# The per-layer gate's product by seven block products, 512 columns wide, with the order of three engines by hand

## The chip, the cores and the metric

The kernel runs on one core of a Trainium2 chip. The metric is the device time of one execution in microseconds. Each kernel is run several times; the median stands for it. Besides, one execution is recorded by the hardware profiler, and the profile's numbers are of that one.

Engines of a core: PE (TensorE, matrix products and transposes through the identity; PEld is its weight load), DVE (VectorE), ACT (ScalarE), POOL (GpSimd), and SP, which here only issues DMAs.

## The reference

One decoder layer for a prompt of 1024 tokens and a sample of 8 sequences of 8 tokens, D_MODEL 1024, all in float32. Of its parts, mixer, MLP with convolution and per-layer input, the change touches the last, with the row scales that it needs:

```python
y, conv_new = conv_ffn(rmsnorm(h, lw['g_ffn']), conv_prev, lw)
h = h + y
h = h + (p.astype(h.dtype) @ lw['ple_w_proj']) * jax.nn.sigmoid(rmsnorm(h, lw['g_ple']) @ lw['ple_w_gate'])
```

`h` is 1024 x 1024 for the prompt (and 64 x 1024 for the sample), `p` 1024 x 256, `ple_w_proj` 256 x 1024, `ple_w_gate` 1024 x 1024. The norm's gain `g_ple` stands on the channels, so it is multiplied into the rows of the gate's weights; the norm's scale of a token is applied inside the sigmoid.

## The kernel before

Every product of full precision is made of three in a reduced format (`mm3`, lines 146 to 149): both operands are split into a high part, a cast that ACT makes (line 123), and a low part, the difference that DVE makes (line 124); high x high, high x low and low x high are summed in PSUM. Line numbers 147 to 149 in the profile are those three matmuls wherever they are used, and 123 and 124 are the split wherever it is used. A tile has 128 tokens (partitions); there are `NT` = 8 of them.

**The stage ahead: the MLP's down product** (lines 2196 to 2378). It is made by seven block products over halves of tokens and columns (`SEVEN`, line 2196), each of eleven steps `k` (`NK`), for four tiles `t` with 512 columns. `load` (2204) brings a step's rows and weights, `operands` (2217) makes its operands in a ring of four rooms `o` (2186), `summed` (2242) issues the matmuls into four PSUM banks `ps_dn`, `folded` (2253) adds a finished product to `h`. Product 4 is the last of the seven; its steps 9 and 10 are summed together, tile by tile (lines 2349 to 2355), and `folded` of it completes `h` for the tokens of tiles 4 to 7 and the first 512 columns. The loop's lines 2361 to 2378 put parts of the gate's stage between steps: `row_scale` (squares of `h` on ACT, line 1470; sum and root on POOL, 1483 and 1484), `turned` (eight transposes of a tile of `h` on PE, line 140, and its split into `xg`), `ple_gate(0)` and `ple_in` (the per-layer input `p`, transposed and split, `pT`).

**The gate's stage** (lines 2383 to 2463). The pool `wf` of the stage ahead is closed and `pl` opened in its place, so that a tile of `pl` waits for the users of the tile of `wf` on whose memory it lies. From the bottom `wf` holds: a small room `fd` (2 KB of each partition), the ring's room `o0` (8 KB), three rooms of 2 KB with tag `stage` (used by the gate's raw weights and by the pieces `pin` of `p`), then `o3`, `o1`, `o2`. `o0` is read by step 9 of product 4; the first of the `stage` rooms is last read by the transposes of the second `pin` of the sample.

The stage runs over four column parts `c` of 256. For each, `ple_proj` (2400) loads and splits 256 columns of `ple_w_proj`, `ple_gate` (2287) loads those of `ple_w_gate` in four pieces, multiplies them by `g_ple` (`gk`) and splits them: ACT line 2298, DVE line 2299. `ple_unit` (2403) does two tiles at a time: 48 matmuls of 256 columns into `ps_pg` (2 tiles x 8 blocks of 128 channels x 3), two sigmoids on ACT (2416), 12 matmuls into `ps_pj2` (line 2419; the profile names that tile `ps_pj`), the product of both and the sum with `h` on DVE (2421, 2422), and the store into `y_p` (2423). `ple_sample` (2425) does the sample's 64 tokens with 20 matmuls (2436), folding high and low tokens, which stand side by side in one operand. Tiles 4 to 7 are transposed inside the stage (2455 to 2458), `conv_out` (2387) turns and stores the convolution's state there.

PSUM has eight banks: `pd` (line 194) is a ring of three, `pm` (200) of two, `p2t` (1640) of two, `p2` (1643) one. `both` (1648) goes round through them. A bank is given out again when all that read its last tile are done.

The order of each engine is made by the scheduler from the program's order and its estimate of times, except in a section under `tc.manual_schedule`, which keeps the order in which the program issues the named engines' work. Before, one such section exists (`PASSAGE`, line 32, used in lines 2108 to 2110), far ahead of the gate. Instructions of the program ahead of such a section may still run between those of the section. All DMAs of this stage are issued by SP, in one queue, in the scheduler's order; an instruction of SP whose wait isn't over holds those behind it.

Of the kernel before, what the change touches and what calls it, by code (L numbers as in the profile page):

```python
# [52 lines left out]
def step_kernel(ctx: ExitStack, tc: tile.TileContext, A):  # L53
# [2110 lines left out]
    oring = [0]  # L2164

    def raws():
        return z["xs"].tile([P, 2, 512], F32, tag="r", name="raw2", bufs=5)

    def xrooms(t):

        for e in range(2):
            n = t * 2 + e
            if n < NK:
                yield z["xs"].tile([P, 8, P], F32R, tag=place_of(n), name="xg", bufs=1)
            else:
                yield z["xs"].tile([P, 8, P], F32R, tag="r", name="xg", bufs=5)

    def turned(t):
        if t == NT:
            z["xss"] = xss = z["fb"].tile([P, 8, P], F32R, tag="xss", name="xss")  # L2180
            transpose_split(p2t, hs, R, lambda c0: tuple(xss[:, c0:c0 + 4, s * R:(s + 1) * R] for s in range(2)))
            return
        xg[t] = tuple(xrooms(t))
        transpose_split(p2t, hrows(t), P, lambda c0: tuple(x[:, c0:c0 + 4] for x in xg[t]))
# [102 lines left out]
    def ple_gate(c):  # L2287

        hl = []
        for i in range(2):  # L2290
            hi, lo = ((z["pl"] if c % 2 else z["fq"]).tile([P, 4, 256], F32R, tag="gu" + s, name="gu" + s, bufs=2) for s in "hl")
            for k0 in (0, 2):
                raw = stg([P, 2, 256], F32)
                r0 = (4 * i + k0) * P
                sp.dma_start(raw, A["ple_w_gate"][0][r0:r0 + 2 * P, c * 256:(c + 1) * 256].rearrange("(k p) c -> p k c", p=P))
                for k in range(2):
                    gk = z["gk"][:, 4 * i + k0 + k:4 * i + k0 + k + 1]
                    act.activation(hi[:, k0 + k], raw[:, k], AF.Copy, scale=gk)
                    dve.scalar_tensor_tensor(lo[:, k0 + k], raw[:, k], gk, hi[:, k0 + k].bitcast(F32), ALU.mult, ALU.subtract)
            hl.append((hi, lo))  # L2300
        return hl

# [37 lines left out]
    pT, wpl = [], None  # L2340
    for i, (p, k) in enumerate(steps):
# [9 lines left out]
        for t in range(4):  # L2351
            for k_ in ((k - 1, k) if p == 4 and k == NK - 1 else (k,)):
                summed(p, k_, t)
            if k == NK - 1:
                folded(p, t)
        if q and k in (1, 3, 5, 7):
            folded_on(q, k // 2)
# [10 lines left out]
        elif p == 1 and k == 7:  # L2368
            turned(NT)
        elif p == 2 and k == 8:  # L2370
            wpl = ple_gate(0)
        elif p == 4:
            if k in (1, 3, 5, 7):
                row_scale(k // 2)
            if k in (2, 4, 6, 8):
                turned(k // 2 - 1)
            if k in (5, 7):
                pT.append(ple_in(k // 7))
    for t in (4, 5):
        row_scale(t)  # L2380

# [18 lines left out]
    def ple_proj(c):  # L2400
        return wload(z["pl"], A["ple_w_proj"][0][:, c * 256:(c + 1) * 256], 2, 256, "wj", 2, st=stg)

    def ple_unit(c, ts, ws):

        c0 = c * 256
        cs = slice(c0, c0 + 256)
        (wj, wg), n = ws, len(ts)
        pg, pj = both([P, 2, 256], "ps_pg"), both([P, 2, 256], "ps_pj2")
        sg = z["pl"].tile([P, 2, 256], F32, tag="sg", name="sg", bufs=3)
        for i, t in enumerate(ts):  # L2410
            xh, xl = xg[t]
            for k in range(8):
                wh, wl = (w[:, k % 4] for w in wg[k // 4])
                mm3(pg[:, i], xh[:, k], xl[:, k], wh, wl, k == 0, k == 7)
        for i, t in enumerate(ts):
            act.activation(sg[:, i], pg[:, i], AF.Sigmoid, scale=z["rs"][:, t:t + 1])
        for i, t in enumerate(ts):
            for k in range(2):
                mm3(pj[:, i], *(x[:, t * P:(t + 1) * P] for x in pT[k][:2]), wj[0][:, k], wj[1][:, k], k == 0, k == 1)
# [92 lines left out]
```

## Time and profile before

| | |
|---|---|
| median of 3 runs | 2200.72 us (2198.4 to 2200.74) |
| the profiled execution | 2198.3 us |
| its span in the profile | 2196.6 us |
| granted PE clock, mean | 0.99 of full |
| bytes read, written (HBM) | 188.00 MB, 42.52 MB |
| last matmul of the product ahead begins | 2063.62 us |
| first matmul of the gate begins | 2063.86 us |
| last matmul of the gate begins | 2192.61 us |

A profiled execution's time counts from start to end on the device; the span runs from the first to the last recorded instruction. An instruction's row gives its start, its duration, engine, line, operation, output and inputs, and in brackets the idle time of its engine just before it with what ended that. On all engines an instruction may begin before the one ahead has ended, so the price of one in a row of many is the step from start to start, not its duration. A view by stretches gives the busy time of each engine in a part of the span.

### The profile page before, as it was taken

What the parts mean: (1) busy time and instruction counts of PE and PEld (TensorE: products, weight loads), DVE (VectorE), ACT (ScalarE), POOL (GpSimd) and SP (SyncE); (2) the same over time, 40 slices, a digit from 0 to 9 for tenths busy, and PEclk for the clock granted to TensorE, in tenths of its full rate; (3) what the DMA queues carried; (4) which work ended last, traced back from release to release, by engine and by line L of the source; (5) the groups of instructions that cost most, each with busy time, mean ns of one, the idle gap of its engine ahead of it and who ended that gap; (6) DMA issues with size and microseconds to landing.
All of it is one profiled execution on the core that took longest, in us unless ns stands there. A gap on an engine that the chain in (4) does not pass through costs nothing.

```text
span 2196.6 us, 38367 instructions
## 1 busy us (share of the span) xinstructions
PE 2125.2 (97%) x13484; PEld 1929.4 (88%) x13484; DVE 1654.9 (75%) x2546; ACT 1363.5 (62%) x3721; POOL 1207.0 (55%) x1311
## 2 busy tenths in 40 slices
PE   7999999999999999999999999999999999999999
PEld 6888978878888888887798978999999999888899
DVE  4675767367778888887788888888888886887642
ACT  5676767777778888887777776443433333534631
POOL 5675668576677777767455556556565662001100
PEclk9899999999999999999999999999999999999999
DMA  5343244422342222221421223232322225778321
GB/s 183 111 142 111 70 126 155 133 68 61 104 121 68 61 68 64 61 65 42 164 91 56 69 77 115 92 106 88 103 84 97 92 91 202 237 222 233 101 72 39
DMA packets 204418, 233.07 MB, mean 106 GB/s; under 512 B 42422, under 2 KB 146339, under 8 KB 204227
## 3 DMA queue, kind: packets, MB, share of 16 engines
q1 hardware_dynamic: 187971, 178.44, 26.0%
...
q14 instruction: 83, 0.68, 0.1%
HBM read 188.00 MB, written 42.52 MB: 105 GB/s over the span
## 4 chain that ended last, share of the span: by engine, by line
PE 81%; DVE 8%; ACT 5%; DMA 3%; issue 1%; POOL 1%; SPq 0%; DVEq 0%; ACTq 0%; POOLq 0%
PE ps_gu L147 7%; PE ps_gu L148 7%; PE ps_gu L149 7%; PE ks L147 5%; PE ks L149 4%; PE ks L148 4%; PE ps_dn L148 3%; PE ps_dn L149 3%; PE ps_dn L147 3%; PE cpv L656 2%; PE ctp L530 2%; PE ps_lt L286 2%; DVE css L573 2%; PE ps_pj L147 2%; PE ps_pj L148 1%
## 5 line engine op out<-in xcount | busy, mean ns | idle before, releaser
L568 ACT ACTIVATE csq<-ks 128x256 f32<-128x256 f32 x1040 | 392.5, 400 | 92.6 <-PE ks L149 80.0
L573 DVE TENSOR_REDUCE css<-csq 128x16 f32<-128x1024 f32 (+1 forms) x264 | 315.8, 1196 | 58.9 <-ACT csq L568 56.1
L123 ACT CAST wh<-st 128x512 fp32r<-128x512 f32 x164 | 100.9, 619 | 165.5 <-PE ps_gu L148 155.9
L147 PE MATMUL ks<-mv0h,cTh 128*128 128x320 f32 (+1 forms) x520 | 171.0, 331 | 9.1 <-ACT sn L570 5.0
L147 PE MATMUL ks<-mv1h,cTh 128*128 128x320 f32 (+1 forms) x520 | 170.5, 330 | 7.7 <-ACT sn L570 3.6
L613 POOL TENSOR_TENSOR chl<-craw,chl 128x1024 fp32r<-128x1024 f32 x64 | 141.0, 2203 | 57.3 <-ACT chl L611 56.4
L148 PE MATMUL ks<-mv1l,cTh 128*128 128x320 f32 (+1 forms) x520 | 153.8, 298 | 0.0
L148 PE MATMUL ks<-mv0l,cTh 128*128 128x320 f32 (+1 forms) x520 | 152.1, 294 | 0.0
L149 PE MATMUL ks<-mv1h,cTl 128*128 128x320 f32 (+1 forms) x520 | 148.9, 300 | 0.1
L149 PE MATMUL ks<-mv0h,cTl 128*128 128x320 f32 (+1 forms) x520 | 147.6, 296 | 0.9 <-DVE cTl L124 0.8
L641 POOL TENSOR_TENSOR phl<-sn,phl 128x512 fp32r<-128x512 f32 (+1 forms) x63 | 84.1, 1335 | 83.5 <-ACT phl L638 83.2
L124 DVE TENSOR_TENSOR wl<-st,wh 128x512 fp32r<-128x512 f32 x124 | 108.7, 879 | 27.6 <-ACT wh L123 27.4
L148 PE MATMUL ps_dn<-o 128*128 128x512 f32 x308 | 120.2, 390 | 0.1
L149 PE MATMUL ps_dn<-o 128*128 128x512 f32 x308 | 120.2, 390 | 0.0
L124 POOL TENSOR_TENSOR wl<-st,wh 128x512 fp32r<-128x512 f32 x40 | 62.6, 1564 | 104.4 <-ACT wh L123 104.4
L124 DVE TENSOR_TENSOR cTl<-ctp,cTh 128x512 fp32r<-128x512 f32 (+1 forms) x136 | 90.1, 662 | 38.7 <-ACT cTh L123 37.8
L147 PEld LDWEIGHTS ks<-mv0h,cTh 128*128 128x128 f32 x520 | 97.9, 188 | 23.8 <-ACT sn L570 10.2
L147 PEld LDWEIGHTS ks<-mv1h,cTh 128*128 128x128 f32 x520 | 99.6, 192 | 19.9 <-ACT sn L570 7.7
L570 ACT COPY sn<-ks 128x64 f32<-128x64 f32 x520 | 116.7, 224 | 0.0
L1318 POOL TENSOR_TENSOR pl<-p,ph 128x512 fp32r<-128x512 f32 (+1 forms) x96 | 97.4, 1019 | 32.2 <-DVE ph L1317 22.0
L147 PE MATMUL ps_dn<-o 128*128 128x512 f32 x308 | 112.8, 390 | 0.0
L149 PE MATMUL ps_gu<-xrh,wl 128*128 128x320 f32 x352 | 108.8, 309 | 0.0
...
## 6 DMA issues: line engine op xcount, KB each, us to landing
...
```

The lines of the kernel that those rows point to most:

```text
L123: cast = act.copy(hi, src)
L124: res = (lo_eng or dve).tensor_tensor(lo, src, hi.bitcast(F32), ALU.subtract)
L147: pe.matmul(ps, ah, bh, start=first, stop=False)
L148: pe.matmul(ps, ah, bl, start=False, stop=False)
L149: return pe.matmul(ps, al, bh, start=False, stop=last)
L286: pe.matmul(ps, x, w, start=first, stop=last)
L568: act.activation(sq[:, f * 256:f * 256 + 256], ks[:, 0:256], AF.Square)
L570: act.copy(o.sn[:, g0 + i, :], ks[:, 256:320])
L573: dve.tensor_reduce(o.ss[:, g0 + i + 1 - n:g0 + i + 1, :].rearrange("p i h -> p (i h)"), sq2[:, :n].rearrange("p i (h n) -> p (i h) n", n= ...
L613: pool.tensor_tensor(ch[:, c0:c1, 128:256], src, ch[:, c0:c1, 0:128].bitcast(F32), ALU.subtract)
L641: (dve if drain == 2 else pool).tensor_tensor(phl[:, :nt, 64:128], sb, phl[:, :nt, 0:64].bitcast(F32), ALU.subtract)
L1318: pool.tensor_tensor(pl[:, c0:], p[:, c0:], ph[:, c0:].bitcast(F32), ALU.subtract)
```

## The change

The product of the gate, h times W (1024 x 1024 by 1024 x 1024, W with the gain in its rows), is cut in halves of tokens, channels and columns, h into H11, H12, H21, H22 (first index tokens, second channels) and W into W11 to W22 (first index channels, second columns), and made of seven block products in place of eight:

- sums of h: S1 = H21 + H22, S2 = S1 - H11, S3 = H11 - H21, S4 = H12 - S2
- sums of W: T1 = W12 - W11, T2 = W22 - T1, T3 = W22 - W12, T4 = W21 - T2
- P1 = H11 W11, P2 = H12 W21, P3 = S4 W22, P4 = H22 T4, P5 = S1 T1, P6 = S2 T2, P7 = S3 T3
- outputs: C11 = P1 + P2; with U2 = P1 + P6 and U3 = U2 + P7: C21 = U3 + P4, C22 = U2 + P5 + P7, C12 = U2 + P5 + P3

A unit `P`*n* *t* is product *n* for tile *t* of four: 4 blocks of 128 channels x 3 matmuls of 512 columns. (`P33` is cut into two halves of 256 columns.) Four banks BA (`pm`, `pm`, `p2t`, `p2t`) or BB (three of `pd`, and `p2`) take a product's four tiles.

The sums of `h` are formed after the transposition, from the transposed tiles: `Y`, `Tb`, `Ta` transpose H22, H21, H12 into banks of `pd` (four transposes each); H11 is turned earlier, in product 4 of the stage ahead (`turn_first`), with a plain copy `r11` kept. `ry`, `ra`, `U` are ACT's copies of transposed tiles and of P1 into `h`; the places of `h` that are overwritten so are stored ahead in a scratch tensor `dh2` (12 stores of 256 KB) and loaded again for the outputs (`hy`, `ha`, `hb`). DVE forms `e` (S1), `i` (S3), `g` (S2), `j` (S4); the splits are `ac`/`al`, `ic`/`il`, `ec`/`el`, `gc`/`gl`, `jc`/`jl`, `yc`/`yl`, with `c` ACT's cast and `l` DVE's difference.

The sums of W are formed from raw weights which are loaded again for each use: `W`, `X`, `V`, `N` (two blocks of 128 channels each), `C`, `Z` (two pieces of 256 KB for one block each). DVE forms `c` (T3), `z` (T1), `v` (T2), `n` (T4), after ACT's scaling `cs`, `zs`; splits as above, `wc`/`wl`, `xc`/`xl` and so on. `JL`, `jc0_`, `jl0_` and `jc1_`, `jl1_` load and split the halves of `ple_w_proj`. All loads but `N` go round through four rooms (`pair`). The new rooms of `pl`, from the bottom: `sg` (8 KB), `wjh` and `wjl` (4 KB each, for `jc0_` and `jl0_`), then the gate's operands and one of the four pair rooms.

Outputs: `Cq`, `Cv`, `Cw`, `Cx` form C11, C22, C21, C12 (DVE), `Cs` is the sigmoid, `J` the projection (6 matmuls of 512), `Cm`, `Ca` product and sum on DVE, `Co` the store. `sA`, `sB`, `sC` (8, 8 and 16 matmuls of 512 columns) and `sJ` (4) are the sample's, with `pA`, `so`, `sx`, `sc`, `sl`, `ss`, `sd`, `sk`, `sm`, `sa` behind them.

PE, ACT, DVE and POOL do the stage in the order of a list `LAST` of 354 names; SP's order is left to the scheduler. Squares of tiles 4 to 7 move into product 4 (the second halves) and right behind it (the first halves), `ple_in(1)` behind the first tile of product 4's last step. `conv_out` uses one bank and one room for its four transposes.

The diff, cut to its core:

```diff
+LAST = (
+    "JL0 jc0_ W0 jl0_ wc0 W1 wc1 wl0 wl1 wc2 C0 wc3 wl2 wl3 C1 cs0 c0 cc0 cl0 cs1 C2 c1 P10 cc1 cl1 Y0 Tb0 cs2 Ta0 "
+    "C3 i0 ry0 P11 c2 ac0 ra0 e0 ic0 g0 cc2 al0 Y1 U0 Tb1 cl2 Z0 ry1 Ta1 i1 P12 cs3 e1 U1 g1 ic1 ac1 j0 ra1 Y2 al1 "
+    "Tb2 ec0 V0 c3 Ta2 ry2 P13 j1 ac2 il1 U2 al2 cc3 il0 ra2 Y3 ec1 cl3 Z1 ry3 i2 el1 ic2 el0 il2 e2 g2 Tb3 ec2 Ta3 "
+    "e3 U3 sA ac3 i3 ec3 al3 ic3 J10 g3 pA el3 ra3 J11 el2 j3 P20 z1 j2 zs1 il3 v1 J12 gc0 z0 vc1 Cq0 zs0 P21 gl0 "
+    "Cs10 v0 vl1 vc0 Cm10 gc1 vl0 J13 gl1 Cq1 P22 N0 Ca10 Cs11 Cm11 Ca11 P23 Co10 gc2 Cq2 gl2 Cs12 Z2 n0 n1 sB gc3 "
+    "Cq3 gl3 Cs13 Co11 Cm12 sJ0 zc1 Ca12 zc0 P70 zl1 sd0 Co12 zl0 z2 V1 so zs2 Cm13 zc2 yc0 Ca13 P71 sc0 zl2 Co13 "
+    "yl0 v2 Z3 sk0 vc2 sl0 yc1 P72 vl2 ss0 yl1 hy0 sm0 z3 P73 N1 yc2 sa0 zs3 yl2 zc3 v3 zl3 cv vc3 hy2 nc0 vl3 yc3 "
+    "n3 JL1 P60 nc1 n2 nc3 nl1 nc2 nl3 cvc hy1 P61 nl0 nl2 jc0 X0 yl3 jl0 P62 u0 jc1 u1 jl1 ha0 P63 X1 u2 jc2 jl2 "
...
+    "Cm23 Co32 Ca23 sJ1 Cm33 Co23 Ca33 sC sd1 Co33 sk1 P30 sx sc1 sl1 ss1 J40 Cx0 sm1 Cs40 P31 sa1 Cm40 Ca40 Co40 "
+    "J41 Cx1 Cs41 P32 Cm41 Ca41 Co41 J42 Cx2 Cs42 J43 Cm42 Ca42 P33 Co42 Cx3 Cs43 Cm43 Ca43 Co43 ")
...
+    def pair():
+
+        pool_, tag = ((z["hp"], "gb"), (z["pl"], "pc"), (z["xs"], place_of(10)), (z["xs"], "r4"))[pairs[0] % 4]
+        pairs[0] += 1
+        return pool_.tile([P, 2, 512], F32, tag=tag, name="wp", bufs=1)
...
+    def unit(ps, x, w, cs=slice(0, 512)):
+
+        for k in range(4):
+            mm3(ps[:, cs], x[:, 0, k], x[:, 1, k], w[k][:, 0, cs], w[k][:, 1, cs], k == 0, k == 3)
+
+    BA, BB = (pm, pm, p2t, p2t), (pd, pd, pd, p2)
...
+        later(f"P1{t}", prod("P1", "11", "11", BA))
+        later(f"P2{t}", prod("P2", "12", "21", BA))
+        later(f"P7{t}", prod("P7", "S3", "T3", BB))
+        later(f"P6{t}", prod("P6", "S2", "T2", BA))
+        later(f"P5{t}", prod("P5", "S1", "T1", BA))
+        later(f"P4{t}", prod("P4", "22", "T4", BA))
+        later(f"w{t}", lambda: dve.tensor_tensor(part(1, 0, t), part(1, 0, t), out["P7", t], ALU.add))
+        later(f"P3{t}", prod("P3", "S4", "22", BA))
+
+        def tb():
+            out["b", t] = turn_part(1, 0, t, pd)
+
+        def ta():
+            out["a", t] = turn_part(0, 1, t, pd)
+
+        def ty():
+            out["y", t] = turn_part(1, 1, t, pd)
...
+        def proj():
+            bank = {1: pd, 2: BA[2 * (t % 2)], 3: pd, 4: BA[2 * (t % 2)] if t > 1 else pd}[n]
...
+    with tc.manual_schedule(engines={pe.engine, act.engine, dve.engine, pool.engine}):
+        for name in LAST.split():
+            todo.pop(name)()
+    assert not todo, todo
-    ws = ple_proj(0), wpl
-    for c in range(4):
-        last = c == 3
-        nxt = None
-        for n, ts in enumerate(((0, 1), (2, 3), None, (4, 5)) + (((6,), (7,)) if last else ((6, 7),))):
-            if ts:
-                ple_unit(c, ts, ws)
-            else:
-                ple_sample(c, ws)
...
-        ws = nxt
```

More of the change, by code (lines that the diff above doesn't have):

```diff
@@ L1610, in step_kernel @@
     dh = [dhp[t * P:(t + 1) * P, :] for t in range(NT)] + [dhs]
+    dh2 = dram.tile([T, D], F32, name="dh2")
     ds = [dram.tile([P, T], F32, name=f"ds{f}") for f in range(NF)]
@@ L2163, in step_kernel @@
     xg = {}
-    oring = [0]
+    oring, rring = [0], [0]
     def raws():
[L2167 to L2174, printed above, removed]
-            else:
[L2176 to L2184, printed above, removed]
+        rring[0] = (rring[0] + 1) % 5
+        return z["xs"].tile([P, 2, 512], F32, tag=f"r{rring[0]}", name="raw2", bufs=1)
@@ new lines, in turned_sample, with part, kept, v4 @@
+    def turned_sample():
+        z["xss"] = xss = z["fb"].tile([P, 8, P], F32R, tag="xss", name="xss")
+        transpose_split(p2t, hs, R, lambda c0: tuple(xss[:, c0:c0 + 4, s * R:(s + 1) * R] for s in range(2)))
+    def part(i, j, t):
+        return h[:, 4 * i + t, j * 512:j * 512 + 512]
+    def kept(i, j, t):
+        return dh2[(4 * i + t) * P:(4 * i + t + 1) * P, j * 512:j * 512 + 512]
+    def v4(x):
+        return x.rearrange("p (k n) -> p k n", n=P)
+    def turn_part(i, j, t, bank, here=False):
+        pt = bank([P, 4, P], "pt")
+        for k in range(4):
+            m = pe.transpose(pt[:, k], part(i, j, t)[:, k * P:(k + 1) * P], ident)
+            if here and k == 0:
+                tc.keep_in_program_order(m)
+        return pt
@@ L2285, in ple_gain @@
         act.copy(z["gk"], pt[:, 0:8])
[L2287 to L2301, printed above, removed]
     def ple_in(c):
@@ L2324, in ple_in @@
         return th, tl, ts
-    z["xs"].tile([P, 2, 512], F32, tag="r", name="raw2", bufs=5)
+    for k in range(5):
+        z["xs"].tile([P, 2, 512], F32, tag=f"r{k}", name="raw2", bufs=1)
     for k in (10, 9, 8):
@@ L2374, in step_kernel @@
                 row_scale(k // 2)
[L2375 to L2380, printed above, removed]
+                square(k // 2 + 4, 1)
+            if k in (2, 4, 6, 7):
+                turn_first((k - 1) // 2)
+            if k in (6, 8):
+                for t in range(4):
+                    i_ = (8 - k) // 2
+                    sp.dma_start(kept(i_, 1, t), part(i_, 1, t))
+            if k == 5:
+                pT.append(ple_in(0))
+    for t in range(4):
+        square(t + 4, 0)
+        root(t + 4)
+        sp.dma_start(kept(1, 0, t), part(1, 0, t))
     rw.close()
@@ new lines, in proj_part, with load_, hi, lo @@
+    def proj_part(f):
+        def load_():
+            raw["jl", f] = x = pair()
+            sp.dma_start(x, A["ple_w_proj"][0][:, f * 512:f * 512 + 512].rearrange("(k p) c -> p k c", p=P))
+        def hi():
+            raw["wj", f] = w = [(z["xs"].tile([P, 2, 512], F32R, tag=place_of(s), name="wj", bufs=1) if f else
+                                 z["pl"].tile([P, 2, 512], F32R, tag="wj" + "hl"[s], name="wj", bufs=1)) for s in range(2)]
+            act.copy(w[0], raw["jl", f])
+        def lo():
+            w = raw["wj", f]
+            dve.tensor_tensor(w[1], raw["jl", f], w[0].bitcast(F32), ALU.subtract)
+        later(f"JL{f}", load_)
+        later(f"jc{f}_", hi)
+        later(f"jl{f}_", lo)
@@ L2400, in ple_proj @@
[L2400 to L2419, printed above, removed]
-        t0 = ts[0]
-        dve.tensor_tensor(sg[:, :n], sg[:, :n], pj[:, :n], ALU.mult)
-        dve.tensor_tensor(sg[:, :n], sg[:, :n], h[:, t0:t0 + n, cs], ALU.add)
-        sp.dma_start(A["y_p"][t0 * P:(t0 + n) * P, cs].rearrange("(i p) c -> p i c", p=P), sg[:, :n])
```

307 lines of the change are left out of this document (267 added, 40 removed), and 3 rows, old and new, of the table LAST.

## The prediction

> **What bounds the kernel now.** I read the page first (engines, slices), then the busy time by stretches around the per-layer gate, then single rows of PE, DVE and ACT there.
>
> ```profile
> span 2196.6 us, 38367 instructions
> ...
> PE 2125.2 (97%) x13484; PEld 1929.4 (88%) x13484; DVE 1654.9 (75%) x2546; ACT 1363.5 (62%) x3721; POOL 1207.0 (55%) x1311
> ```
>
> ```profile
> 2032.00:2063.80 31.80, 31.80 (x155) 26.27 (x154) 20.64 (x27) 17.65 (x36) 6.49 (x9) 1.00 0.25 79
> 2063.80:2193.00 129.20, 129.09 (x1098) 128.64 (x1097) 48.94 (x88) 42.39 (x95) 2.46 (x6) 1.00 0.22 69
> 2193.00:2196.60 3.60, 0.00 (x0) 0.00 (x0) 0.83 (x2) 0.00 (x0) 0.00 (x0) 0.84 0.11 36
> ```
>
> In each row stand the stretch, its length, then busy time of PE, PEld, DVE, ACT, POOL, the granted clock, DMA share and GB/s. The gate's stage is the second row: PE is busy for 129.09 of 129.20 us at full clock, DVE for 48.94. So PE's work is the stage's length, and DVE has 80 us to spare. The third row is the tail after PE's last matmul.
>
> What one matmul costs is read from start to start, since busy times overlap:
>
> ```profile
> 1981.33 0.39 PE L147 MATMUL ps_dn<-o 128*128 128x512 f32 x1
> ...
> 1983.37 0.39 PE L147 MATMUL ps_dn<-o 128*128 128x512 f32 x1
> ...
> 2100.58 0.28 PE L147 MATMUL ps_pg<-guh,xg 128*128 128x256 f32 x1
> ...
> 2106.06 0.28 PE L149 MATMUL ps_pg<-guh,xg 128*128 128x256 f32 x1
> 2106.18 0.28 PE L147 MATMUL ps_pj<-wjh,ph 128*128 128x256 f32 x1
> ...
> 2107.62 0.28 PE L147 MATMUL ps_pg<-guh,xg 128*128 128x256 f32 x1
> ```
>
> and, from the chain of work that ended last (start, length, what):
>
> ```profile
> 2092.55 0.44 PE pt L140 x4
> ...
> 2145.86 2.40 PE ps_pg L2436 x20
> ```
>
> Nine 512-wide matmuls of the product before take 2.04 us, 0.2267 each. The 48 gate matmuls of one unit take 47 steps of 5.48 us in all, 0.1166 each; twelve `ps_pj` take 1.44 us, 0.120 each; four transposes 0.44 us; the sample's twenty 2.40 us, 0.120 each.
>
> **The change, PE's work.** Removed: 768 gate matmuls of 256 columns (8 tiles x 8 blocks x 3 x 4 column parts), 768 x 0.1166 = 89.5 us. Added: 7 products x 4 tiles x 12 = 336 of 512 columns; the last unit is cut in two, so 324 x 0.2267 + 24 x 0.1166 = 76.2 us. Gain 13.3, of which 10.9 is the missing eighth product (48 x 0.2267) and the rest width. Projection: 192 x 0.120 - 96 x 0.2267 = 1.3. Sample: 80 x 0.120 - 40 x 0.2267 = 0.5. Transposes: 64 for the prompt before and after, 48 of them now inside the new stage (5.3 us). **PE's work falls by 15.1 us**; the listed PE order then holds 112.7 us.
>
> By the Trainium skill, "TensorE: Matmul & The Clock Gate", section "Wait — 56ns, not 53.3ns?", a warm matmul steps at N/2.4 GHz + 2.5 ns, which is 109 ns for 256 columns and 216 ns for 512; by that width would save only 2.5 ns a pair, and the sum would be an estimated 11.7 us. The rows (116.6 and 226.7 ns) differ, and they decide.
>
> **The change, DVE and the start of the stage.** The hand-written list has 152 DVE instructions, against 88 in the stage before. Their prices:
>
> ```profile
> 2029.06 1.22 DVE L124 TENSOR_TENSOR o<-raw,o 128x1024 fp32r<-128x1024 f32 x1
> 2030.20 0.68 DVE L2230 TENSOR_TENSOR raw<-raw,st 128x512 f32<-128x512 f32 x1
> 2030.80 1.88 DVE L2268 TENSOR_TENSOR h<-h,ps_dn 128x512 f32<-128x512 f32 x3
> ...
> 2039.61 1.07 ACT L123 CAST xg<-pt 128x512 fp32r<-128x512 f32 x2
> ...
> 2079.83 0.48 DVE L2299 SCALAR_TENSOR_TENSOR gul<-stg,gkT,guh 128x256 fp32r<-128x256 f32 x1
> ...
> 2098.49 1.68 DVE L2299 SCALAR_TENSOR_TENSOR gul<-stg,gkT,guh 128x256 fp32r<-128x256 f32 x4 [2.83 <-ACT guh L2298]
> ...
> 2185.95 0.69 DVE L2421 TENSOR_TENSOR sg<-sg,ps_pj 128x512 f32<-128x512 f32 x1 [4.36 <-PE ps_pj L149]
> ...
> 2186.67 0.69 DVE L2422 TENSOR_TENSOR sg<-sg,h 128x512 f32<-128x512 f32 x1
> ```
>
> A 512-wide sum or difference steps at 0.60 us when the next doesn't need it (three in 1.88), at 0.72 when it does (2185.95 to 2186.67), a 1024-wide one at 1.14. Four scaled differences of 256 take 1.68, 0.40 each; I put 512 at 0.67 (0.60 plus the 0.06 by which 0.48 exceeds the 0.42 of a plain sum of 256, quoted with the tail; bounds 0.60 and twice 0.40). The whole list is then some 95 us: 20 x 0.67, two of 1.14, 130 of 0.61. That fits under 112.7 on average, but order decides.
>
> PE's three transposes of a tile (`Y`, `Tb`, `Ta`) go through `pd`, a ring of three banks, so `Tb3` takes the bank of `Tb2` and waits for its last reader, `e2`. Ahead of `Tb3` PE has four units and ten groups of transposes: 4 x 2.72 + 10 x 0.44 = 15.3 us. Up to and with `e2` DVE has 31 instructions: 1.14 + 8 x 0.67 + 22 x 0.60 = 19.7 us. When does DVE begin?
>
> ```profile
> 2059.73 0.48 SPq L2314 DMA_DIRECT2D pin<-p_sample  x1
> 2063.36 7.73 SPq L165 DMA_DIRECT2D stg<-ple_w_proj  x2
> 2064.05 0.69 DVE L2268 TENSOR_TENSOR h<-h,ps_dn 128x512 f32<-128x512 f32 x1 [0.68 <-PE ps_dn L149]
> 2066.20 0.63 ACT L1470 ACTIVATE junk<-h 128x512 bf16<-128x512 f32 x1
> ```
>
> The pool `pl` lies on the rooms of `wf`. SP's first load into it stands until 2063.36, the end of the last product, and the second of the pair about 7 us longer, for the room of the sample's `pin`. `wjh`, which the list's first ACT step `jc0_` writes, lies on those same two rooms, and ACT, DVE keep their order: `jl0_` and all behind it wait. So DVE starts about 0.8 us after PE's first unit (the fold's 0.69 and a hand-over; bounds 0 and 3, the latter if `pin` is turned late). Two pairs `c0`/`cc0`/`cl0`, `c1`/`cc1`/`cl1` hand over between DVE and ACT with little between them: 0.7 us idle each. `e2` ends at 0.8 + 19.7 + 1.4 = 21.9, and **PE stands 21.9 - 15.3 = 6.6 us** in pieces before `Tb3`. Smaller holds earlier (`Tb1` on `e0`, `Ta1` on `al0`) are part of it, not added.
>
> Behind that, DVE waits for `P20`, `P22`, `P23` (some 1.8 us in all); `P71`, `P72` then wait for `pd` banks that `Cm13` and `sk0` free: 0.7 us more. `P60` needs `vl3`, at 52.0 us of DVE's list, for its last quarter at 50.3 of PE's; with the holds above it comes in time. Behind `P60` DVE has 43 us of list, PE 60: nothing waits again. ACT's list of 94 steps is some 53 us (two 512-wide copies end in 1.07) and hidden behind PE's throughout.
>
> SP moves 8.4 + 1 MB of weights in place of 4.2, stores `dh2` (3 MB) and loads it back: in the stage some 70 issues of 0.4 us, and about 18 MB in 118 us, 150 GB/s, where 69 is moved now. Four pair rooms in a ring: `C1` may start when `jl0_` is done and is wanted 4 us later. I cost this at nothing, covered by DVE's work ahead of each use; if that cover goes, each late pair costs DVE up to 3 us.
>
> Ahead of the stage, in the last product's stretch (DVE 20.64, ACT 17.65 of 31.80), the earlier squares, four copies `r11` and eight stores into `dh2` come in, and four halves of `xg` go out: nothing, hidden behind PE's 31.80; some 0.6 us each if not. `conv_out` in one bank: nothing, since its stores bound nobody.
>
> **The tail.**
>
> ```profile
> 2192.22 0.47 ACT L2416 ACTIVATE sg<-ps_pg,rs 128x256 f32<-128x256 f32 x1 [3.00 <-PE ps_pg L149]
> ...
> 2192.61 0.28 PE L149 MATMUL ps_pj<-wjh,pl 128*128 128x256 f32 x1
> 2192.99 0.42 DVE L2421 TENSOR_TENSOR sg<-sg,ps_pj 128x256 f32<-128x256 f32 x1 [2.64 <-PE ps_pj L149]
> 2193.44 0.42 DVE L2422 TENSOR_TENSOR sg<-sg,h 128x256 f32<-128x256 f32 x1
> 2193.93 0.34 SPq L2423 DMA_DIRECT2D y_p<-sg  x1
> ```
>
> Now two DVE steps and a store follow the last matmul. After, sum, sigmoid (0.47), product, sum follow it, in two halves interleaved on DVE: **+1.5 us** (bounds 1.0 and 2.0).
>
> **Sum.** -15.1 + 6.6 + 0.7 + 1.5 = **-6.3 us**, against the profiled execution's 2198.3 (span 2196.6). The median of the runs shown is 2200.72, 2.4 above it; taken from the median: **2194.4 us**.
>
> **The clock**, as a cost that I leave at nothing:
>
> ```profile
> 1287.90:1291.30 3.40, 0.91 (x5) 0.67 (x5) 3.40 (x5) 2.30 (x8) 0.78 (x1) 0.94 0.01 2
> 1291.30:1294.70 3.40, 3.40 (x17) 3.40 (x18) 1.60 (x4) 1.76 (x7) 1.42 (x1) 0.56 0.01 2
> ```
>
> After 3.4 us in which PE worked 0.91, the next 3.4 are granted 0.56. Between `P11` and `P12` PE would work 1.3 of 5.4 us, so one such stretch is likely; it falls on `P12` and `P13`, while PE waits for DVE anyway. Without that cover it costs 1.7 us. The Trainium skill, "TensorE: Matmul & The Clock Gate", section "HAM oscillation — how this bites in real kernels", wants a gap of over 3.4 us for it; the row shows that a mostly idle stretch is enough.
>
> **Rivals.** The rows they need (the first from the timeline, the others from the list of waits: total, times, longest):
>
> ```profile
> 2102.18 1.74 ACT L2298 ACTIVATE guh<-stg,gkT 128x256 fp32r<-128x256 f32 x4 [0.78 <-DMA stg<-ple_w_gate]
> ```
> ```profile
> DVE gul L2299 <- ACT guh L2298: 6.5, 4, 2.8
> ...
> DVE xg L124 <- ACT xg L123: 4.6, 3, 2.9
> ```
>
> 1. *No stall.* If `jc0_`'s room comes free early, DVE starts 5 us or more before PE's first unit, as it has time to do in the first quoted stretch (20.64 busy of 31.80): -15.1 + 1.5 = **-13.6, 2187.1 us**. Against it: the 2063.36 row. Chance 0.15.
> 2. *Late loads.* `kept` stores, pair loads and reloads share SP's one queue. Two or three pairs, or `V1` and `Z3` in a row ahead of `P60`, come 2 to 3 us late: 3 to 8 us, **2197.4 to 2202.4**. For it: ACT's gate cast waits for its load already now (0.78 us). Against: DMA's low share, 0.22. Chance 0.22.
> 3. *DVE is the bound, slower.* If hand-overs make DVE step at 0.80 us, not 0.61, `vl3`, its 83rd instruction, comes 83 x 0.19 = 15.8 us later and holds `P60`: 52.0 + 15.8 + 2.2 - 50.3 = 19.7 us (2.2 being the start and the two early hand-overs), so -15.1 + 19.7 + 1.5 = +6.1, **2206.8 us**. It decides from a step of 0.73 on (a hold of 13.6 us, no gain left), and is slower by 0.2% from 0.78. For it: the 0.72 of dependent pairs, and DVE's waits for ACT's first halves (6.5 us in four). Against: dependent pairs are a minority of the list, and four scaled differences beside ACT's casts step at 0.40. Chance 0.11.
> 4. *It doesn't do what it says*: 512 columns cost as much as twice 256 here. Then the gain is 4.0 us less (336 x 0.0065 + 96 x 0.0133 + 0.5): 2198.4. The rows of the product before speak against it. Chance 0.02.
>
> **Chances.** My forecast (2191 to 2197.5) has 0.50. Its low end is from a start at 0 and a short tail, its high end from a start at 3 us. The range leaves out the far parts of rivals 2 and 3 and keeps most of rival 1: **2186.5 to 2201.5**. About 0.2%, 4.4 us, is what a measurement of this kernel can tell from no change. Faster: 0.43 of the forecast's 0.50, rival 1, 0.02 of rival 2: 0.60. Same: 0.07 + 0.20 + 0.02 = 0.29. Slower: rival 3, 0.11.
>
> **What would show it.** Right: in the new stage, the matmuls step at 0.227; PE idles some 6 us between `P10` and `sA`, its releaser DVE's `e`, `al` or `i` steps; after `P60` none; DVE is busy above 80% up to `P60`; the tail is about 5 us. Wrong: PE idle with a DMA as releaser (rival 2), a wait of `P60` on DVE's `vl3` (rival 3), no idle at all (rival 1).

## The result and the profile after

The changed kernel takes **2208.88 us** (median of 8 runs, 2206.66 to 2212.72) against 2199.68 (2196.78 to 2206.68) before, measured beside it: ratio **1.0041**, 95% interval 1.0028 to 1.0053. It is slower by 9.2 us, where 6.3 less were predicted.

The page of the changed kernel, span and engines:

```profile
span 2205.2 us, 37408 instructions
...
PE 2117.2 (96%) x12928; PEld 1897.3 (86%) x12928; DVE 1701.4 (77%) x2611; ACT 1384.4 (63%) x3735; POOL 1207.0 (55%) x1311
```

PE has fewer instructions and less busy time than before (2125.2), yet the span is longer. The busy time by stretches (columns as in the prediction) says where. The first row is the gate's stage from P10's first matmul on, the second the tail, the others pieces of the stage:

```profile
2061.30:2199.90 138.60, 121.65 (x546) 97.51 (x544) 99.80 (x155) 61.16 (x105) 1.73 (x4) 0.94 0.36 116
2199.90:2205.20 5.30, 0.00 (x0) 0.00 (x0) 2.23 (x6) 0.91 (x2) 0.00 (x0) 0.92 0.15 49
...
2069.50:2080.50 11.00, 0.07 (x1) 0.07 (x2) 7.99 (x12) 7.37 (x13) 0.00 (x0) 0.58 0.62 188
2080.50:2084.00 3.50, 3.31 (x13) 2.60 (x14) 3.46 (x7) 3.50 (x8) 0.00 (x0) 0.50 0.45 161
...
2121.80:2126.10 4.30, 0.00 (x1) 0.03 (x1) 1.49 (x3) 0.71 (x2) 0.00 (x0) 0.97 0.49 187
2126.10:2129.00 2.90, 2.90 (x7) 2.32 (x8) 2.90 (x6) 1.16 (x2) 0.00 (x0) 0.50 0.63 193
2129.00:2199.60 70.60, 70.60 (x318) 57.40 (x317) 47.20 (x71) 21.75 (x36) 0.00 (x0) 1.00 0.29 96
```

Before, PE was busy in 129.09 of 129.20 us; now it is idle for 17 of 138.6, 15.3 of it in two gaps, and behind each gap PE works for some 3 us at half clock (0.50). Behind the second PE never waits again. From the list of waits of PE in this stage (total, times, longest):

```profile
PE pt L2201 <- ACT h L2542: 11.2, 2, 11.0
PE ps_pg L161 <- ACT wg L2494: 4.3, 1, 4.3
PE ps_pj L161 <- DVE sg L2603: 0.9, 1, 0.9
```

**The first gap**, in the timelines of PE, ACT and DVE (line 137 and 138 are now the split, 2364 the transposes of `pin`, 2542 `ry`, 2635 `cs`, 2674 and 2678 `jc` and `jl`, 2503 `wl`):

```profile
2069.16 0.27 PE L2364 MATMUL pt_pl<-ident,pin 64*128 64x64 f32 x1
2080.43 2.09 PE L2201 MATMUL pt<-ident,h 128*128 128x128 f32 x8 [10.99 <-ACT h L2542]
...
2069.47 0.21 ACT L137 CAST pts<-pt_pl 128x64 fp32r<-128x64 f32 x1 [2.73 <-PE pt_pl L2364]
2069.58 1.05 ACT L2674 CAST wj<-wp 128x1024 fp32r<-128x1024 f32 x1
...
2079.18 0.72 ACT L2635 ACTIVATE wp<-wp,gkT 128x512 f32<-128x512 f32 x1 [1.27 <-DMA wp<-ple_w_gate]
2079.81 0.57 ACT L2542 COPY h<-pt 128x512 f32<-128x512 f32 x1
...
2070.66 1.23 DVE L2678 TENSOR_TENSOR wj<-wp,wj 128x1024 fp32r<-128x1024 f32 x1 [0.72 <-ACT wj L2674]
2071.80 2.73 DVE L2503 SCALAR_TENSOR_TENSOR wg<-wp,gkT,wg 128x512 fp32r<-128x512 f32 x4
```

PE stands at `Y1`, which wants the bank that `ry0` frees. `ry0` is one copy of 0.57 us on ACT, whose input `Y0` was transposed 15.7 us earlier (2064.10), but in the hand's order it stands behind `jc0_`, `wc0` to `wc3`, `cs0`, `cc0`, `cs1`, `cc1` and `cs2`. That row of steps begins at 2069.58, right behind the split of the sample's rows (`pts`), and these were turned on PE only behind P11 (2069.16). So DVE's list begins 9.4 us after P10, not 0.8, and ACT's reaches `ry0` 18.5 us after P10.

**The second gap**, in the timelines of SP, DVE and PE (2631 the pairs, 2647 `N`, 2669 `JL`, 2638 `v`):

```profile
2112.91 0.81 SPq L2631 DMA_DIRECT2D wp<-ple_w_gate  x2
2114.37 0.38 SPq L2647 DMA_DIRECT2D wn<-ple_w_gate  x1
2115.70 0.34 SPq L2613 DMA_DIRECT2D y_p<-sg  x1
2116.30 0.38 SPq L2669 DMA_DIRECT2D wp<-ple_w_proj  x1
2116.90 0.38 SPq L2631 DMA_DIRECT2D wp<-ple_w_gate  x1
...
2124.61 0.75 DVE L2638 SCALAR_TENSOR_TENSOR wp<-wp,gkT 128x512 f32<-128x512 f32 x1 [4.01 <-DMA wp<-ple_w_gate]
...
2126.10 0.76 PE L161 MATMUL ps_pg<-wg,xg 128*128 128x512 f32 x1 [4.31 <-ACT wg L2494]
2126.66 0.63 PE L162 MATMUL ps_pg<-wg,xg 128*128 128x512 f32 x1
2127.09 0.63 PE L163 MATMUL ps_pg<-wg,xg 128*128 128x512 f32 x1
```

The last of the five issues is `V1`. It is used 7.7 us later; `Z3`, `N1`, a store and `JL1` went just ahead (v1_first below shows that this is why); `v2` waits for it, and P60 for `v2`'s high part.

**The balance** of the stage from P10's first matmul to the end of the span. The span begins and ends with other things, and P10 begins between 2061.3 and 2068.2 in the executions shown here, so this length is what the experiments below are compared by, beside the times. It was 132.7 us (2063.86 to 2196.6) and is 143.9 (2061.30 to 2205.2): +11.2. PE's idle time +16.9; half clock an estimated +3.5 (the rows at 0.50 hold 3.3 and 2.9 us of work, of which half is lost, and some of it lies before and behind them); the tail 5.6 against 4.0 (from the start of the last matmul), +1.6. PE's work itself is what is left, -10.8; it wasn't measured apart from the half clock. The span grew by 8.6 us only, since P10 began 2.6 us earlier in this execution, less than it varies from one to another.

### The profile page after: what moved, and what is told of

Read it like the earlier page. It is cut to its first block, busy times and chain, and to the rows that moved or that the text cites. A ratio compares the mean times of both kernels' runs of the same rounds, so it can differ in the third digit from the quotient of the medians.

```text
span 2205.2 us, 37408 instructions
## 1 busy us (share of the span) xinstructions
PE 2117.2 (96%) x12928; PEld 1897.3 (86%) x12928; DVE 1701.4 (77%) x2611; ACT 1384.4 (63%) x3735; POOL 1207.0 (55%) x1311
```

## The experiments

All are set against the kernel before, measured beside them. Short diffs are against the changed kernel, those of order2 and order3 against order and order2; "stage" is the length just defined, in the one execution profiled, while a ratio is of medians.

**rooms.** Does DVE start late because of the memory under `wjh` and `wjl`?

```diff
-    for s in "hl":
-        z["pl"].tile([P, 2, 512], F32R, tag="wj" + s, name="wj", bufs=1)
-    for q in ("q30", "q31", "q32", "q33", "q20", "q21", "q22", "q23"):
-        wroom2(z["pl"], q)
+    for q in ("q30", "q31", "wjh", "wjl", "q32", "q33", "q20", "q21", "q22", "q23"):
+        if q[0] == "w":
+            z["pl"].tile([P, 2, 512], F32R, tag=q, name="wj", bufs=1)
+        else:
+            wroom2(z["pl"], q)
```

> Only the rooms change: wjh and wjl no longer lie on the last operand and on the blocks of p, but on an operand read 5 us earlier. Theory 1a (DVE's list starts late because jc0_ waits for its room): DVE starts some 6 us earlier, the 11.0 us in which PE stands before Y1 shrink to about 5, and the time falls by 6 to 8 us against the changed kernel, to about 2201 to 2203. Theory 1b (it starts late because the split of the sample's rows, whose transposes come on PE only after P11, stands ahead of it in ACT's and DVE's order): no difference, within 2 us of the changed kernel. Rival, DVE's pitch is the bound: no difference either.

Ratio 1.0045 (1.0029 to 1.0062), stage 142.8, first gap 10.8 us: no difference. While the sample's split stands ahead, the room isn't what holds DVE; theory 1a falls, and with it the reason that the prediction gave for the start.

**pin_early.** Does the split of `p` hold it, by its place in the engines' order?

```diff
-            if p == 4 and k == NK - 1 and t == 0:
-                pT.append(ple_in(1))
...
-            if k == 5:
-                pT.append(ple_in(0))
+            if k in (1, 3):
+                pT.append(ple_in(k // 2))
```

> Only the place of the splitting of p changes: both halves, with the sample's rows, are transposed and split during the last product (steps 1 and 3 of it) instead of 5 and 7. Theory 1b: ACT and DVE are free for the list when the last operand has been read, at about 2061; the load W0, which SP issues behind the four stores into dh2, lands some 4 us later and then sets wl0: DVE's four wl come at 2066 instead of 2071.8, PE's gap before Y1 shrinks from 11.0 to about 5, and the time falls by 5 to 7 us, to about 2202 to 2204. Theory 1a alone (the room, without the order) expects the same here, so this run tells only whether the pin matters. Rival, late loads hold the start (C1 and C2 land at 2074 to 2079 whatever DVE does): gap at least 9 us, time within 2 us of the changed kernel.

Ratio 1.0026 (1.0015 to 1.0037), stage 136.8 (some 1 us of its 7.1 are nine transposes that now come ahead of P10). Its waits of PE:

```profile
PE pt L2201 <- ACT h L2540: 5.2, 2, 4.9
PE ps_pg L161 <- ACT wg L2492: 3.0, 1, 3.0
```

The gap fell from 11.0 to 4.9, as theory 1b said. The rooms are the old ones here, and yet `jl0_` begins 1.3 us behind P10 (2065.01 against 2063.67), not 9.4. The time fell by 3.3 us by the ratios, less than the stage and less than the 5 to 7 that were expected; the two intervals together leave room for about 0 to 7.

**start_early** adds to it the rooms of the first run and a turned ring, so that `W0` loads early (in pin_early ACT waits 1.98 us for it).

```diff
-        pool_, tag = ((z["hp"], "gb"), (z["pl"], "pc"), (z["xs"], place_of(10)), (z["xs"], "r4"))[pairs[0] % 4]
+        pool_, tag = ((z["hp"], "gb"), (z["xs"], place_of(10)), (z["xs"], "r4"), (z["pl"], "pc"))[pairs[0] % 4]
```

> The splitting of p early, wjh and wjl on an operand read earlier, and the ring of pair rooms turned so that W0 and W1 load before the stores into dh2 and C0 behind them. Theory 1 (the start is all of the first gap): DVE's list starts about 1 us after P10 begins, near the 0.8 us of the prediction, PE's gap before Y1 shrinks from 11.0 to 3 to 5 us, with it goes the stretch at half clock behind it, and the time falls by 8 to 11 us, to about 2198 to 2201. Rival, loads: C0 to C2 now come in a row and each holds DVE by 2 to 3 us: the gap stays at 7 or more, and the time falls by less than 5 us.

Ratio 1.0024 (1.0013 to 1.0035), stage 136.6. DVE's list again begins 1.3 us after P10 (2065.18 against 2063.84), and in DVE's timeline `V1` is still late:

```profile
2065.18 1.23 DVE L2677 TENSOR_TENSOR wj<-wp,wj 128x1024 fp32r<-128x1024 f32 x1 [0.46 <-ACT wj L2673]
...
2119.64 0.75 DVE L2637 SCALAR_TENSOR_TENSOR wp<-wp,gkT 128x512 f32<-128x512 f32 x1 [3.37 <-DMA wp<-ple_w_gate]
```

PE's waits between P10 and `sA` are 4.4 us (3.6, 0.4, 0.2, 0.2): with nearly the start that the prediction assumed, two thirds of its 6.6 us for that place came about, though before `Y1` and behind ACT. The second gap stays at 3.7 us, and both gaps are still followed by half clock. The time fell by 3.7 us by the ratios, where 8 to 11 were expected and the stage shows 7.3; this difference stays open.

**v1_first.** `N1` and `JL1` are issued behind `V1`.

```diff
-                    sp.dma_start(x[:, m * n:(m + 1) * n], gate_src(i_, j_, k_, n))
+                    raw["ld", key] = sp.dma_start(x[:, m * n:(m + 1) * n], gate_src(i_, j_, k_, n)).ins
...
-                sp.dma_start(x, gate_src(1, 0, k, 2))
+                with tc.issue_after(raw["ld", ("V", j)]) if j else nullcontext():
+                    sp.dma_start(x, gate_src(1, 0, k, 2))
...
-            sp.dma_start(x, A["ple_w_proj"][0][:, f * 512:f * 512 + 512].rearrange("(k p) c -> p k c", p=P))
+            with tc.issue_after(raw["ld", ("V", 1)]) if f else nullcontext():
+                sp.dma_start(x, A["ple_w_proj"][0][:, f * 512:f * 512 + 512].rearrange("(k p) c -> p k c", p=P))
```

> Only SP's order changes: N1 (512 KB) and the second half of the projection's weights (512 KB) are issued behind V1, not ahead of it. Theory 2 (P60's wait of 4.3 us is V1's load, held up by what stands ahead of it in SP's queue and in the rings): V1 lands some 3 us after its issue instead of 7.7, the wait before P60 falls to 1 us or less, with it the half clock behind it (some 1.3 us), and the time falls by 3 to 5.5 us, to about 2203.5 to 2206. Rival, DVE's pitch: v2 is late anyway, as the list ahead of it is, and the time stays within 1.5 us of the changed kernel.

Ratio 1.0025 (1.0013 to 1.0037), 3.5 us less than the changed kernel; stage 138.7. DVE's `v2` begins 4.0 us behind the issue of `V1` (2119.73 and 2123.72), not 7.7. The wait before P60 falls to 0.6 us, and the first gap isn't touched:

```profile
PE pt L2201 <- ACT h L2542: 10.9, 2, 10.6
...
PE ps_pg L161 <- ACT wg L2494: 0.6, 1, 0.6
```

**start_v1** is both.

> The early start and V1 ahead of N1 and JL1 together. Theory: the two gaps are separate causes and add. Of the stage from P10's first matmul to the last recorded instruction (143.9 us in the changed kernel, 136.6 with the early start, 138.7 with V1 first) some 132 us are left; PE's wait before P60 falls from 3.7 to under 1 us, the gap before Y1 stays at 3.6, and the time is 2197 to 2200, within 0.2% of the kernel before. Rival, they share one cause (DVE late as a whole): P60 still waits 2 us or more for DVE, and the stage stays at 134.5 us or more.

Ratio 1.0003 (0.9994 to 1.0011), stage 132.2: the two causes add, and give back what the change had cost, but no more. Left are the first gap's 3.7 us and the half clock behind it.

**order** writes the list anew up to P71, on top of start_v1 (its beginning, before and after):

```diff
-    "JL0 jc0_ W0 jl0_ wc0 W1 wc1 wl0 wl1 wc2 C0 wc3 wl2 wl3 C1 cs0 c0 cc0 cl0 cs1 C2 c1 P10 cc1 cl1 Y0 Tb0 cs2 Ta0 "
-    "C3 i0 ry0 P11 c2 ac0 ra0 e0 ic0 g0 cc2 al0 Y1 U0 Tb1 cl2 Z0 ry1 Ta1 i1 P12 cs3 e1 U1 g1 ic1 ac1 j0 ra1 Y2 al1 "
...
+    "JL0 jc0_ W0 jl0_ wc0 W1 wc1 wl0 wl1 wc2 C0 wc3 wl2 wl3 C1 C2 C3 P10 Y0 Tb0 Ta0 ry0 i0 P11 ac0 e0 ra0 ic0 al0 Y1 "
+    "U0 Tb1 ry1 Ta1 g0 i1 P12 cs0 e1 ac1 U1 ic1 al1 ec0 ra1 g1 c0 Y2 cc0 Tb2 il0 Ta2 ry2 cl0 Z0 P13 el0 ac2 U2 i2 "
...
```

> As the run before, and the order of DVE and ACT written anew up to P71: the differences c1 to c3, j0 to j3 and their low parts, which nothing needs before P70, go behind e3, and what frees the banks of the transposes (ry, i, e, al) comes first; sB is moved between J11 and P20. Theory (what is left of the first gap is order: c0 to c2 with their loads and hand-overs stand ahead of e0): PE's idle time between P10 and sA falls from some 4.8 us to under 2, no stretch at half clock is left there, which cost some 2.5 us more, and the stage from P10 to the end takes 127 to 129 us: the time is 2192 to 2196, below the kernel before. Rival, DVE has too much to do up to P70 in any order: the idle time comes back before P70 or P60, 3 us or more, and the stage stays at 131 us or more.

Ratio 1.0000 (0.9991 to 1.0008), stage 131.9. The first gap is gone entirely, but in PE's timeline it has come back before P70, P71 and P60:

```profile
2107.58 0.50 PE L161 MATMUL ps_pg<-wg,xg 128*128 128x512 f32 x1 [3.99 <-DVE sg L2602]
...
2114.54 0.50 PE L161 MATMUL ps_pg<-wg,xg 128*128 128x512 f32 x1 [2.35 <-DVE sg L2602]
...
2119.53 0.47 PE L161 MATMUL ps_pg<-wg,xg 128*128 128x512 f32 x1 [0.39 <-ACT wg L2493]
```

The rival was right: DVE, late with `Cm12` and `Cm13`, holds the banks. A gap closed by putting work off returns where the work is due.

**order2** puts off what P60 doesn't need, and gives `Z3` the room of `Z1`.

```diff
-    "vc1 Ca10 Cq1 Cs11 Co10 z0 zs0 P22 Cm11 el3 v0 vl1 gc1 Ca11 Co11 vc0 gl1 N0 J13 vl0 Cq2 Cs12 P23 gc2 zc1 Cm12 "
-    "gl2 zc0 n0 Ca12 Co12 n1 Cq3 Cs13 sJ0 so gc3 zl1 zl0 V1 z2 zs2 Cm13 gl3 P70 sd0 zc2 yc0 Ca13 P71 sc0 zl2 Co13 "
...
+    "Cs11 z0 zs0 vl1 v0 vc0 P22 Cm11 gc1 Ca10 Co10 J13 vl0 Cq2 Cs12 gl1 gc2 P23 Cm12 zc1 gl2 zc0 zl0 V1 zl1 Z3 Cq3 "
+    "Cs13 Ca11 Co11 sJ0 so z2 Cm13 gc3 P70 zs2 sd0 gl3 P71 sk0 yc0 v2 vc2 Ca12 Co12 P72 vl2 z3 zs3 Ca13 Co13 P73 v3 "
...
-        pool_, tag = ((z["hp"], "gb"), (z["xs"], place_of(10)), (z["xs"], "r4"), (z["pl"], "pc"))[pairs[0] % 4]
+        pool_, tag = ((z["hp"], "gb"), (z["xs"], place_of(10)), (z["xs"], "r4"), (z["pl"], "pc"))[PAIRS[key]]
```

> As the run named order up to J11; behind it what P60 doesn't need (n0, n1, zl2, zl3, yl0 to yl2, j2, j3, some stores) goes behind P60, what frees the banks for P70 and P71 (Cm12, Cm13) and what V1 and Z3 load into (zl0, zl1) comes earlier, and Z3 takes Z1's room. Theory (with the early start DVE is the bound from P10 to P60, and the 6.7 us of waits in the run named order, with some 3.5 us of half clock behind them, are what its list has too much before P60): PE's idle time in the whole stage falls to under 3 us, the stage from P10 to the end takes 124 to 127 us against 131.9, and the time is 2191 to 2194.5. Rival, the waits are the loads' (V1, Z3) or ACT's sigmoids, not DVE's load: 4 us or more of idle time stay, with a DMA or ACT as releaser, and the stage takes 129 us or more.

Ratio 1.0010 (1.0001 to 1.0019), stage 133.4: worse, where 124 to 127 were expected. No wait is left before P60, as the theory wanted (2.8 us in two waits for `Cm12` and `Cm13` stay). But the list had a new fault, which PE's timeline names:

```profile
2134.52 0.80 PE L161 MATMUL ps_pg<-wg,xg 128*128 128x512 f32 x1 [6.18 <-ACT cst L2768]
```

P63's bank holds the convolution's state until ACT has copied it out, and I had put that copy behind steps that wait for `N1`.

**order3** mends that.

```diff
-    "vc3 j0 cv vl3 j1 P60 zc2 sc0 zl2 yl0 N0 sl0 zc3 ss0 zl3 sm0 yc1 sa0 yl1 hy0 n0 n1 JL1 nc0 nc1 yc2 P61 nl0 nl1 "
-    "j2 j3 N1 yl2 hy1 yc3 n2 n3 nc2 nc3 cvc P62 u0 nl2 nl3 X0 yl3 jc0 hy2 jl0 u1 jc1 jl1 ha0 P63 X1 u2 jc2 jl2 P50 "
+    "vc3 j0 cv vl3 j1 P60 sc0 j2 sl0 j3 ss0 N1 zc2 sm0 zl2 sa0 cvc yl0 N0 zc3 zl3 yc1 yl1 hy0 n0 n1 JL1 nc0 nc1 yc2 "
+    "P61 nl0 nl1 yl2 hy1 yc3 n2 n3 nc2 nc3 P62 u0 nl2 nl3 X0 yl3 jc0 hy2 jl0 u1 jc1 jl1 ha0 P63 X1 u2 jc2 jl2 P50 "
```

> As the run named order2, with cvc right behind the sample's last steps, so that P63's bank is free in time, and N1 and its differences earlier. Theory: the 6.2 us before P63 and the some 2.2 us of half clock behind them go, the stage from P10 to the end takes 124 to 126 us, and the time is 2190 to 2194.5. Rival, the waits move on to P50 or P40 (their gates' low parts come later now): idle time of 3 us or more behind P60, and a stage of 128 us or more.

Ratio 0.9982 (0.9973 to 0.9991), stage 126.1, PE's idle time 2.8 us in all: just inside what was expected. By hand, the change can be made to gain 4.4 us.

**no_hand.** The seven products with the scheduler's own order of all four engines in place of the list.

```diff
-    with tc.manual_schedule(engines={pe.engine, act.engine, dve.engine, pool.engine}):
+    with nullcontext():
         for name in LAST.split():
```

> The seven products as in the changed kernel, but with the scheduler's own order of the three engines instead of the one written by hand. If the hand's order is what costs (its first steps stand behind the sample's pin), the scheduler's order is better: below 2205. If it saves what I think it does (the scheduler takes the list as it stands for all engines but fills gaps by its own estimate of times), it is slower than the changed kernel by more than 2 us: 2211 or more. In between the order by hand is worth nothing.

Ratio **0.9979** (0.9968 to 0.9989), stage 128.4: better than the hand's by 15.5 us of stage and, by the ratios, 13.6 us of time. So the hand's order saves nothing here; it costs. Its waits of PE, and rows of its ACT, PE and DVE (P10 begins at 2067.26):

```profile
PE ps_pg L162 <- DVE wg L2501: 2.6, 1, 2.6
PE ps_pg L163 <- DVE xg L2483: 1.0, 1, 1.0
PE ps_pj L161 <- DVE sg L2603: 0.3, 1, 0.3
```

```profile
2070.69 0.59 ACT L2542 COPY h<-pt 128x512 f32<-128x512 f32 x1 [1.56 <-PE pt L2201]
...
2077.15 1.05 ACT L2674 CAST wj<-wp 128x1024 fp32r<-128x1024 f32 x1
...
2075.39 1.41 PE L2687 MATMUL ps_pg<-wg,xss 128*128 128x512 f32 x5
2076.73 0.27 PE L2364 MATMUL pt_pl<-ident,pin 64*128 64x64 f32 x1
...
2078.23 1.23 DVE L2678 TENSOR_TENSOR wj<-wp,wj 128x1024 fp32r<-128x1024 f32 x1 [0.72 <-ACT wj L2674]
```

This is the telling comparison. The projection's split begins even later here, `jl0_` 11.0 us after P10 against 9.4, and the sample's rows are turned as late as ever. But `ry0` (ACT, line 2542) runs 3.4 us after P10 instead of 18.5, ahead of all that. `Y1` follows P11 without a wait, and ahead of `Tb1` PE does the sample's `sA` (line 2687) and part of P12. So the late start needn't make the first gap; it does because the list puts `ry0` and `e0` behind it. It isn't free in this order either: nh_start below takes another 4.9 us out of the stage.

**hand_pe** and **hand_ad**: the hand's order on PE alone, and on DVE, ACT and POOL alone (the set of engines named in the section is `{pe.engine}`, or all but it).

> The changed kernel with PE's order by hand and the scheduler's own order on DVE and ACT. Theory 3 (what costs is the order of PE: Y1, Tb1 and Ta1 stand ahead of P12 and P13, which wait for nothing, so PE is held by whatever DVE and ACT do first): PE still waits before Y1 or Tb1, 4 us or more, and the time is 2203 or more. Theory 4 (what costs is the order of DVE and ACT: ry0 and e0, for which Y1 and Tb1 wait, stand behind the projection's split and the differences c0 to c2): the wait is under 2 us, and the time is 2199 or less.

> The changed kernel with the order of DVE and ACT by hand and the scheduler's own order on PE. Theory 3: PE goes on with P12 and P13 while DVE is late, the 11.0 us before Y1 fall to 5 or less, and the time is 2202 or less. Theory 4: DVE's and ACT's late start stays, PE has only P12 and P13 (5.4 us) to put in between, so 5 us or more of idle time stay in the first 25 us of the stage, the wait for V1 stays as well, and the time is 2202 to 2206.

hand_pe: 1.0027 (1.0010 to 1.0044), stage 134.9. hand_ad: 1.0038 (1.0024 to 1.0052), stage 140.1. The longest of their waits of PE:

```profile
PE pt L2201 <- ACT h L2542: 3.7, 1, 3.7
PE ps_pj L161 <- DVE sg L2603: 2.0, 1, 2.0
PE pt L2201 <- DVE sg L2546: 1.4, 1, 1.4
```

```profile
PE pt L2201 <- ACT h L2542: 5.2, 1, 5.2
PE ps_pg L161 <- DVE sg L2586: 3.7, 2, 2.7
PE ps_pg L161 <- ACT wg L2494: 2.9, 3, 1.7
```

Neither theory is right alone: each half of the list, set against the scheduler's other half, leaves PE waiting. Freeing DVE, ACT and POOL is worth 9.0 us of stage, freeing PE 3.8, both together 15.5. By the times the two are worth only 3.1 and 0.7 us, with intervals that reach the changed kernel's 1.0041; so it is the waits that show it, not the times.

**no_hand_sv**, **nh_start**, **nh_v1**: the scheduler's order with both, the first or the second of the early start and `V1` first.

> The scheduler's own order on all engines, with the early start and V1 ahead of N1 and JL1. Theory (what is left in the run with the scheduler's order, 3.8 us of PE's idle time and some 2 us of half clock, comes from DVE's late start): the idle time falls to under 2 us, the stage from P10 to the end takes 124 to 127 us against 128.4, and the time is 2191 to 2195. Rival, DVE is the bound in the scheduler's order from the start to P60 whatever its start: the stage stays at 127.5 us or more.

> The scheduler's own order with the early start alone (splitting of p early, rooms, ring), without V1 first. If the early start gives the 5.2 us between the scheduler's order alone (stage 128.4) and that with both (123.2): stage 123 to 125, time 2190 to 2192. If V1 does: stage 127 or more, time 2194 or more.

> The scheduler's own order with V1 first alone. If the early start gives the 5.2 us: stage 127 or more, time 2194 or more. If V1 does: stage 123 to 125, time 2190 to 2192. In the scheduler's order V1's wait was not seen in PE's idle time (3.8 us in all, released by DVE's splits), so I expect the first.

| | ratio | stage |
|---|---|---|
| no_hand_sv | 0.9957 (0.9944 to 0.9971) | 123.2 |
| nh_start | 0.9950 (0.9937 to 0.9964) | 123.6 |
| nh_v1 | 0.9989 (0.9980 to 0.9997) | 129.2 |

The early start is all of it (about 1 us of the stage being the nine transposes that come ahead of P10); `V1` first gives nothing once the order is free. With nh_start PE waits 1.7 us in the whole stage, and the kernel takes **2189.99 us**, 0.50% less than before: the best of the versions here, not to be told from no_hand_sv.

**nh_width**: as no_hand_sv, each block product in two halves of 256 columns.

```diff
-                    unit(out[name, t], xg[key, t], gates[w])
+                    for c in (0, 256):
+                        unit(out[name, t], xg[key, t], gates[w], cs=slice(c, c + 256))
```

> As the run with the scheduler's own order, the early start and V1 first (2190.1 us, stage from P10 to the end 123.2), but every block product of the prompt in two halves of 256 columns: 648 matmuls of 256 in place of 324 of 512. Theory 5 (512 columns are cheaper here as in the product before, as the prediction took them: 0.2267 against 2 x 0.1166): at most 2.2 us are lost, and less if the gate's 512-wide units really step at 0.2336. Theory 6 (rival 4 of the prediction, for the block products alone: 0.2336 a step is twice 0.1168, so the width gives nothing there): no difference beyond 1 us in the stage, 122.5 to 124.5. If halves step at 0.120, the stage grows by 2 us or more.

Ratio 0.9968 (0.9956 to 0.9979), stage 125.2, but with 3.2 us of idle time against 1.4; without those 122.0 against 121.8. PE's timeline, 27 steps of 256 columns:

```profile
2149.85 0.28 PE L161 MATMUL ps_pg<-wg,xg 128*128 128x256 f32 x1
...
2152.99 0.28 PE L163 MATMUL ps_pg<-wg,xg 128*128 128x256 f32 x1
```

3.14 / 27 = 0.1163 each. In the changed kernel eleven steps of 512 columns take 2.57 us:

```profile
2061.30 0.40 PE L161 MATMUL ps_pg<-wg,xg 128*128 128x512 f32 x1
...
2063.87 0.39 PE L163 MATMUL ps_pg<-wg,xg 128*128 128x512 f32 x1
```

0.2336 each, twice 0.1168. In the block products width gives nothing; theory 6 holds.

## Why the prediction was wrong, step by step

*"DVE starts about 0.8 us after PE's first unit ... bounds 0 and 3."* **This is the step that failed first and cost most**: it was 9.4 us, and the early start takes 7.3 us out of the stage, `V1` first 5.2. The prediction looked for the wait in the memory under `wjh`; rooms shows that this didn't hold it. What stands ahead in ACT's and DVE's order is the sample's split, and PE's order puts its transposes behind P11. That the bound of 3 us was reserved for "if `pin` is turned late" shows the place was seen, but not what stood between: two units on PE.

*"`e2` ends at 0.8 + 19.7 + 1.4 = 21.9, and PE stands 21.9 - 15.3 = 6.6 us in pieces before `Tb3`."* PE stood before `Y1`, for 11.0 us, on ACT. The chain was drawn through DVE alone; *"ACT's list of 94 steps is some 53 us ... and hidden behind PE's throughout"* was read from ACT's sum (53 us), but an engine kept to a fixed order is late by what stands ahead of the one step that matters, not by its sum. no_hand shows it from the other side: the same sum, the same late split, no gap before `Y1`. Given the early start, 4.4 us of the 6.6 came about (start_early).

*"P60 needs `vl3` ... with the holds above it comes in time"*, and *"SP moves ... I cost this at nothing"*. Wrong by 4.3 us: rival 2, for `V1` as it named it. v1_first shows the load to be the cause. The predicted cover, DVE's work ahead of each use, was there for most other pairs (ACT's `cs2`, ahead of `ry0`, waited 1.27 us for its load); `V1` gets its room late, when three loads and a store are ahead of it. Behind P60 nothing waited, as predicted.

*The clock, left at nothing.* Each gap was followed by some 3 us at half clock, which costs about 3.5 in all and which nothing covered: the stretch falls on the matmuls behind the gap, not on the gap.

*PE's work, -15.1.* It fell by about 10.8. The width term was mis-sized: 336 x (0.2336 - 0.2267) = 2.3 us less (rival 4, right for the block products, given 0.02). Of the other 2, some 0.8 is only how idle time is counted (from a matmul's end, 0.16 us behind its step, five times), and some 0.4 are four transposes of `h` that stood ahead of the stage (20 before, 16 after); the remainder stays open. The Trainium skill, "TensorE: Matmul & The Clock Gate", section "Wait — 56ns, not 53.3ns?", gives an estimated 2.5 ns of gain for a pair of 256 made one of 512. Measured here is a loss of 1.0 ns (2 x 116.3 against 233.6), where the row of the other product had promised a gain of 6.5. The page was nearer than the row that I let decide.

*The tail, +1.5*: +1.6. *DVE's step*: right, 0.60 in rows; rival 3 had no part, since DVE is idle for 4.0 us in front of `v2`; that its 2206.8 lies near the measured time is chance.

So -10.8 + 16.9 + 3.5 + 1.6 = +11.2 for the stage, against -15.1 + 7.3 + 0 + 1.5 = -6.3. The mechanism, seven products for eight, is worth nearly what it promised less the width: in nh_start PE is busy for 116.5 us of the stage against 129.0 before, and the stage is 9.1 us shorter (about 1 us of both being the transposes ahead of P10). The list written by hand gave it back.
